# Score products of a gated linear recurrence: from full 128x128 blocks to 32x32 and 64x64 tiles

## The chip, the core and the metric

One core of one Trainium2 chip runs the whole kernel. The metric is device time in microseconds (us), the median of several runs; a smaller time is better. PE is TensorE's matmul side and PEld its weight loads, DVE is VectorE, ACT is ScalarE, POOL is GpSimd, SP is SyncE, whose queue issues the DMAs.

## The reference, cut to what matters

One layer of a hybrid trunk on 2048 latent tokens of width 1024 with 256 context tokens. A combined projection feeds two head groups, the outputs are projected back, and a gated MLP with a 3x3 depthwise convolution follows. The change is in the first head group: a gated linear recurrence in both directions, with four heads of 128 channels. For one direction it computes

```python
decay = jnp.where(mask, jnp.exp(jnp.where(mask, diff, 0.0)), 0.0)     # diff = b_t - b_s, b the running sum of log gates
scores = jnp.einsum('bhtk,bhsk,bhtsk->bhts', qc, kc, decay)
o = o_inter + jnp.einsum('bhts,bhsv->bhtv', scores, vc)               # o_inter: queries on the state before the chunk
```

The score of a query t and a key s is a sum over 128 channels of q, k and the product of the gates between them. Forward scores have s before t, backward ones t before s, and on the diagonal both directions add up.

## The kernel before, in words

**Scores level by level.** The kernel takes chunks of 128 positions, so a sequence half of 1024 positions (hh = 0 or 1) has eight. In a chunk the scores are made by halving: at level B (1, 2, 4, ... 64) positions are in blocks of B, two neighbouring blocks make a pair, and the scores between the two blocks of a pair are wanted. For these the decay splits into a part on the query side and a part on the key side, so that one plain matrix product gives them. `Q` holds the queries of the two directions, already decayed up to a block's edge, `K` likewise the keys; after each level `level_update` multiplies one half of `Q` by the totals of the blocks (in place, L470 of DVE), `level_keys` writes new keys (multiplications on DVE and POOL, L546 and L537, copies on ACT, L548 and L538), and `next_tot` the totals of the blocks twice as long. The diagonal comes first, from `kd = K[:,0] + K[:,1]` and plain queries `qs`.

**How a level is computed.** `hg` (L719) does this per head and half, so eight times. At each level each of the eight chunks gets one full 128x128 product in fp32 (the keys of the chunk as weights, a view of `Q` as the moving operand, L744), four to a bank of PSUM. Of its 128x128 results only the opposite blocks of the pairs are wanted; DVE copies those into `sc` through a byte mask of that level (`copy_predicated`, L747, 128x512 at a time). The diagonal's products (L731) come first and ACT copies them whole (L732). A product in fp32 is two passes of PE, each a weight load and a matmul; those in fp32r (the projections) are one. At the end `sc` is multiplied with the values (L795), beside the queries on the states.

**What sets the order.** PE's stream between 233 and 996 us is mostly the input projection, `run_banks` (L481): products of 128x512 in fp32r, three for each of eight slices of the contraction. After each slice it calls `slot`, which lets two pumps emit a step of work: `hg_q` (the recurrence) and `bg_q` (modulation blocks, the scaled output and down weights). A step ends with `yield` of a wait, and the next one comes when the model clock `T.t` (which adds up a price for each product, L64) has moved on that far: 4.2 model us between most levels. `need` forces steps ahead of it where the next head wants a buffer. A scheduler then places the emitted instructions on each engine's queue, and semaphores keep them correct. All engines work through their queues in order.

Of the kernel before, what the change touches and what calls it, by code (L numbers as in the profile page):

```python
# [9 lines left out]
F32 = mybir.dt.float32  # L10
F32R = mybir.dt.float32r
BF16 = mybir.dt.bfloat16
U8 = mybir.dt.uint8
# [5 lines left out]
P = 128  # L19
# [3 lines left out]
TH = SEQ // 2  # L23
NCH = TH // P
# [6 lines left out]
RH = TH // GW  # L31
EPS = 1e-6
LV = [1, 2, 4, 8, 16, 32, 64]
AL = 512


# [12 lines left out]
def view(t, off, dims):  # L49

    return bass.AP(t.tensor, t.offset + off, [list(t.ap[0])] + [list(d) for d in dims])


class Tensor:
# [5 lines left out]
    def matmul(self, out, lhsT, rhs, **kw):  # L60
        n = 1
        for _, count in rhs.ap[1:]:
            n *= count
        self.t += n / 2400 + 0.0135 if rhs.dtype == F32R else 2 * max(0.112, n / 1200 + 0.005)  # L64
        return self.engine.matmul(out, lhsT, rhs, **kw)  # L65

    def transpose(self, out, in_, identity):
# [5 lines left out]
def tile_trunk(ctx, tc, x, c, cx, c_ctx, w_ada, b_ada, norm_mix, norm_ffn, w_in, hg_norm, sgu_g, sgu_b,  # L73
               w_sp, b_sp, w_out, w_up, conv_w, conv_b, w_down, norm_final, masks, out):
    nc = tc.nc
    V, S, G, T = nc.vector, nc.scalar, nc.gpsimd, Tensor(nc.tensor)
    ld = nc.sync.dma_start
# [100 lines left out]
    with es1:  # L178
        ps = es1.enter_context(tc.tile_pool(name="ps1", bufs=1, space=PSUM, reuse_waits="tile"))
        p1 = es1.enter_context(tc.tile_pool(name="p1", bufs=1, reuse_waits="tile"))  # L180
        pm = es1.enter_context(tc.tile_pool(name="pm", bufs=1, reuse_waits="tile"))
        pk = esk.enter_context(tc.tile_pool(name="pk", bufs=1, side="right", reuse_waits="tile"))
        ph = esh.enter_context(tc.tile_pool(name="ph", bufs=1, side="right", reuse_waits="tile"))
        wa = [p1.tile([P, NK, TH], F32, tag=t, name="wa", align_bytes=AL) for t in ("xl", "xh")]
        wsT = pm.tile([P, NH, P], F32, name="wsT")
        rh = pm.tile([P, NH, P], F32, name="rh")
        msk = pm.tile([P, 8, P], U8, name="msk")
        hf = [pm.tile([P, P], F32, name=f"hf{h}") for h in range(NH)]
        hb = [pm.tile([P, P], F32, name=f"hb{h}") for h in range(NH)]
        tb0 = [pm.tile([P, NCH], F32, name=f"tb0_{h}") for h in range(NH)]  # L190
# [1 line left out]
        def bank(tag):  # L192
            return ps.tile([P, 512], F32, tag=tag, name=tag, bufs={"pj": 3, "sc": 2, "mi": 3}[tag])
# [230 lines left out]

        def misc():

            for l in range(0, 8, 4):
                mf = pm.tile([P, 4, P], F32, tag="gu", name="mf", bufs=2)
                ld(mf, masks.rearrange("p (l j) -> p l j", j=P)[:, l:l + 4, :])
                V.tensor_copy(msk[:, l:l + 4, :], mf)  # L430
            yield 1.0
            wsr = pm.tile([P, NH, P], F32, tag="nt", name="wsr", bufs=2)
            ld(wsr, w_sp[0].rearrange("h p q -> p h q"))
            bsb = pm.tile([P, NH, P], F32, tag="nt", name="bsb", bufs=2)
            ld(bsb, b_sp[0:1].broadcast_to([P, NH, P]))
            yield 5.0
            pv = bank("mi")
            for h in range(NH):
                T.transpose(pv[:, h * P:(h + 1) * P], wsr[:, h, :], ident)
            V.tensor_copy(wsT, pv.rearrange("p (h q) -> p h q", q=P))  # L440
            yield 2.5
            pv = bank("mi")
            for h in range(NH):
                T.matmul(pv[:, h * P:(h + 1) * P], ones, wsT[:, h, :], start=True, stop=True)
            for h in range(NH):
                V.scalar_tensor_tensor(out=rh[:, h, :], in0=pv[:, h * P:(h + 1) * P], scalar=sgb[:, h:h + 1],
                                       in1=bsb[:, h, :], op0=ALU.mult, op1=ALU.add)
            yield 0.0
# [162 lines left out]
        for h in range(NH):  # L611
            F, K, vt = sets[h % 2]
# [106 lines left out]
        def hg(hh, h, F, K, qs, vt, sgt):  # L719
            kd = ph.tile([P, TH], F32, tag="T1", name="kd")  # L720
            G.tensor_add(kd, K[:, 0, :], K[:, 1, :])
            Q = ph.tile([P, 2, TH], F32, tag="Q", name="Q", align_bytes=AL)
# [1 line left out]
                V.tensor_mul(Q[:, d, :], qs, F[:, d, :])  # L724
            yield 6.5
            sc = ph.tile([P, NCH, P], F32, tag="S", name="sc")
            for g in range(0, NCH, 4):
                pb = bank("sc")
                for i in range(4):
                    sl = slice((g + i) * P, (g + i + 1) * P)  # L730
                    T.matmul(pb[:, i * P:(i + 1) * P], kd[:, sl], qs[:, sl], start=True, stop=True)  # L731
                S.copy(sc[:, g:g + 4, :], pb.rearrange("p (c t) -> p c t", t=P))  # L732
            done.add((hh, h, "diag"))
            yield 3.6
            tot = F
            for l, B in enumerate(LV):
                dims = [[2 * B, P // (2 * B)], [TH + B, 2], [1, B]]
                if B == 1:
                    dims = dims[:2]
                if B == P // 2:  # L740
                    dims = dims[1:]
                for g in range(0, NCH, 4):
                    pb = bank("sc")
                    for i in range(4):  # L744
                        off = (g + i) * P
                        T.matmul(pb[:, i * P:(i + 1) * P], K[:, 0, off:off + P], view(Q, off, dims), start=True, stop=True)
                    V.copy_predicated(sc[:, g:g + 4, :], view(msk, l * P, [[0, 4], [1, P]]),  # L747
                                      pb.rearrange("p (c t) -> p c t", t=P))
                level_update(Q, TH, B, tot, False)
                K = level_keys(K, B, tot)  # L750
                tot = next_tot(tot, TH, B)
                yield (6.5, 5.2)[l] if hh == 0 and l < 2 else 4.2
# [16 lines left out]
            for d, dst, o in ((0, fs, 1), (1, bs_, 0)):  # L769
                for g in range(0, NCH, 4):  # L770
                    pd = bank("mi")
                    for i in range(4):
                        sl = slice((g + i) * P, (g + i + 1) * P)
# [15 lines left out]
            for g in range(0, NCH, 4):  # L789
                po = bank("mi")  # L790
                for i in range(4):
                    ch = g + i
                    sl = slice(ch * P, (ch + 1) * P)
# [266 lines left out]
        i = len(seq) - 4  # L1060
# [394 lines left out]
    for n, (u, i) in enumerate(prods):  # L1455
# [4 lines left out]
        p = ubank()  # L1460
# [275 lines left out]
```

## Time and profile before

| what | value |
|---|---|
| median of 3 runs | 2518.82 us (2515.85 to 2520.11) |
| profiled execution | 2518.86 us, its span 2517.0 us |
| busy share of the span | PE 97%, PEld 80%, DVE 72%, POOL 42%, ACT 38% |
| score products on PE | 896 + 128 passes, 138.0 us busy |
| masked copies L747 on DVE | 112, mean 739 ns, 81.0 us busy |
| stage with the recurrence | about 230 to 1010 us of the span |

In the page, a line of part 5 is a group of equal instructions with its count, busy time, mean duration in ns, the idle time of the engine ahead of them and what ended it. PE's instructions overlap in its pipeline, so a mean duration is longer than the distance between two starts; prices are read from starts. In the timeline the first number is the start and the second the time to the end of the last of the merged instructions, both in us.

### The profile page before, as it was taken

Reading aid. Unit: us, or ns where it says so; the run is one execution under the profiler, and the core shown is the slowest. Engines: PE = TensorE matmul, PEld = TensorE weight load, DVE = VectorE, ACT = ScalarE, POOL = GpSimd, SP = SyncE. Lnnn points to the kernel's source line nnn. Section 1 sums busy time; section 2 is a strip of 40 time slices with the busy share of each in tenths; the row PEclk is TensorE's granted clock in tenths of the full one; section 3 lists DMA queues with packets and bytes.
Section 4 is the critical chain, followed back from the end, with each engine's and each line's share of the span. In section 5 each row is a group of like instructions: output and inputs, shape, how many; then the busy total and the mean of one; then the engine's idle time right before and its main releaser. Section 6 shows DMA issues by size and latency. Waiting matters only on the chain.

```text
span 2517.0 us, 32793 instructions
## 1 busy us (share of the span) xinstructions
PE 2439.9 (97%) x11859; PEld 2021.6 (80%) x11859; DVE 1800.4 (72%) x2367; ACT 959.9 (38%) x1598; POOL 1060.6 (42%) x879
## 2 busy tenths in 40 slices
PE   7999999999999999899999999999999999999998
PEld 4788888878888888688778888878878887888887
DVE  5866766745757657365699787759999993675876
ACT  2554334434344333254443333323333342323243
POOL 1444232322333423100477878878778771000002
PEclk9999999999999999999999999999999999999999
DMA  8355334583342522667942222382222239843744
GB/s 293 101 193 174 116 113 159 176 295 112 126 158 97 176 85 76 234 204 235 313 140 89 86 87 90 104 307 73 91 91 90 87 113 332 294 150 126 257 138 176
DMA packets 305838, 400.13 MB, mean 159 GB/s; under 512 B 33025, under 2 KB 216057, under 8 KB 301965
## 3 DMA queue, kind: packets, MB, share of 16 engines
q1 hardware_dynamic: 302420, 397.30, 47.7%
q8 instruction: 94, 1.54, 0.3%
q10 hardware_dynamic: 3257, 0.75, 0.1%
q14 instruction: 67, 0.55, 0.1%
HBM read 288.85 MB, written 109.13 MB: 158 GB/s over the span
## 4 chain that ended last, share of the span: by engine, by line
PE 38%; DVE 6%; POOL 2%; issue 2%; DMA 2%; ACT 1%; SPq 0%; POOLq 0%; ACTq 0%; DVEq 0%
PE up L65 22%; PE dn L65 17%; DVE dn L1316 3%; DVE edges L1321 1%; POOL Al L121 1%; DMA raw<-in_w_up_dram 1%; DVE gp L1392 1%; ACT dn L1313 0%; DMA yfar<-yd 0%; POOL raw L1142 0%; DVE keep L1402 0%; DVE keep L1386 0%; DMA m<-cv 0%; ACT cv L1335 0%; POOL cv L1403 0%
## 5 line engine op out<-in xcount | busy, mean ns | idle before, releaser
L1316 DVE SCALAR_TENSOR_TENSOR dn<-gp,taps,dn 128x1024 f32<-128x1024 f32 x352 | 448.3, 1280 | 21.0 <-ACT dn L1313 17.8
L65 PE MATMUL up<-yfar,Ah 128*128 128x512 f32 x1232 | 394.4, 390 | 2.2 <-DMA yfar<-yd 2.2
L121 POOL TENSOR_TENSOR Al<-raw,Ah 128x512 fp32r<-128x512 f32 x264 | 343.9, 1311 | 90.1 <-ACT Ah L120 82.9
L65 PE MATMUL dn<-thl,mhl 128*128 128x512 f32 x1680 | 381.0, 389 | 0.0
L65 PE MATMUL pj<-xh,whi 128*128 128x512 f32 x896 | 366.8, 410 | 2.1 <-ACT whi L120 1.6
L65 PEld LDWEIGHTS dn<-thl,mhl 128*128 128x128 f32 x1680 | 315.2, 188 | 65.6 <-issue 0.2
L65 PE MATMUL pj<-xl,whi 128*128 128x512 f32 x896 | 353.6, 395 | 3.7 <-DMA xl<-xl_d 1.8
L65 PE MATMUL pj<-xh,wlo 128*128 128x512 f32 x896 | 353.4, 395 | 2.7 <-POOL wlo L121 1.7
L65 PE MATMUL up<-xah,Al 128*128 128x512 f32 x704 | 275.9, 392 | 2.4 <-POOL Al L121 2.4
L65 PE MATMUL up<-xah,Ah 128*128 128x512 f32 x704 | 275.2, 391 | 1.8 <-ACT Ah L120 1.8
L65 PEld LDWEIGHTS up<-yfar,Ah 128*128 128x128 f32 x1232 | 231.4, 188 | 50.8 <-DMA yfar<-yd 2.6
L120 ACT CAST Ah<-raw 128x512 fp32r<-128x512 f32 x264 | 160.4, 618 | 283.5 <-PE up L65 213.7
L121 POOL TENSOR_TENSOR wlo<-raw,whi 128x1024 fp32r<-128x1024 f32 x56 | 143.8, 2569 | 243.1 <-ACT whi L120 204.0
L65 PE MATMUL up<-xal,Ah 128*128 128x512 f32 x528 | 205.5, 389 | 0.0
L65 PE MATMUL up<-yfar,Al 128*128 128x512 f32 x528 | 205.2, 389 | 0.0
L65 PEld LDWEIGHTS pj<-xh,wlo 128*128 128x128 f32 x896 | 169.7, 189 | 39.5 <-POOL wlo L121 2.1
L65 PEld LDWEIGHTS pj<-xh,whi 128*128 128x128 f32 x896 | 170.0, 190 | 36.9 <-issue 3.8
L65 PEld LDWEIGHTS pj<-xl,whi 128*128 128x128 f32 x896 | 170.0, 190 | 36.1 <-DMA xl<-xl_d 2.8
L65 PE MATMUL dn<-wo,o 128*128 128x512 f32 x768 | 184.9, 397 | 3.4 <-DMA wo<-wo_d 2.1
L65 PEld LDWEIGHTS dn<-wo,o 128*128 128x128 f32 x768 | 143.0, 189 | 33.7 <-DMA wo<-wo_d 2.5
L65 PEld LDWEIGHTS up<-xah,Al 128*128 128x128 f32 x704 | 132.4, 188 | 33.8 <-POOL Al L121 6.4
L65 PEld LDWEIGHTS up<-xah,Ah 128*128 128x128 f32 x704 | 132.6, 188 | 30.2 <-ACT Ah L120 2.8
(320 smaller groups left out, 4077.3 us busy)
## 6 DMA issues: line engine op xcount, KB each, us to landing
raw<-in_w_up_dram SPq DMA_DIRECT2D x88, 512.0 KB
mr<-m SPq DMA_DIRECT2D x85, 512.0 KB
raw<-in_w_in_dram SPq DMA_DIRECT2D x68, 512.0 KB
sT<-wd SPq DMA_DIRECT2D x88, 256.0 KB
raw<-in_w_ada_dram SPq DMA_DIRECT2D x32, 512.0 KB
yfar<-yd SPq DMA_DIRECT2D x14, 1024.0 KB
m<-cv SPq DMA_DIRECT2D x22, 544.0 KB
raw<-in_w_down_dram SPq DMA_DIRECT2D x22, 512.0 KB
```

The costliest lines, as they stand in the source:

```text
L65: return self.engine.matmul(out, lhsT, rhs, **kw)
L120: keep(S.copy(hi, raw))
L121: (eng or G).tensor_sub(lo, raw, hi.bitcast(F32))
L1316: V.scalar_tensor_tensor(out=cr, in0=gt[:, t // 3:t // 3 + RH, t % 3:t % 3 + GW], scalar=taps[:, t * NF + f:t * NF + f + 1], in1=cr, op0=A ...
L1321: V.scalar_tensor_tensor(out=e[:, 0, :], in0=gt[:, 1, t % 3:t % 3 + GW], scalar=taps[:, t * NF + f:t * NF + f + 1], in1=e[:, 0, :], op0=AL ...
L1392: V.tensor_add(g_rows(hh, f + c, n2), quad(p, kind), quad(add, kind))
```

## The change

Only the wanted blocks are computed, as small tiles. A tile takes all 128 rows of the array (the channels) and 32 or 64 of its columns, at the column group that goes with the partitions of its result. For the diagonal and the levels below 32 (`B < SB`) each chunk gets four products 32x32 (keys and queries of the same 32 positions), and the results of all eight chunks lie packed in one bank, 128x256. ACT copies the diagonal's results into a packed tile `near`, DVE merges the levels 1 to 16 into it with a mask of 32 columns. At level 32 the four products of a chunk are the 32x32 blocks off the diagonal, at level 64 there are two of 64x64; ACT copies these into `sc` block by block, and with level 32 also the blocks of `near`. One bank is used per level in place of two. The model clock prices a tile at a share of a pass by its width, which holds for the one- and two-column products of the modulation too. The masks are loaded in four small DMAs in place of two.

```diff
 LV = [1, 2, 4, 8, 16, 32, 64]
+SB = 32
+NB_ = LV.index(SB)
...
-        self.t += n / 2400 + 0.0135 if rhs.dtype == F32R else 2 * max(0.112, n / 1200 + 0.005)
+        if lhsT.ap[1][1] < P and out.ap[0][1] == lhsT.ap[1][1]:
+            self.t += 2 * lhsT.ap[1][1] / P * max(0.03, n / 1200 + 0.005)
+        else:
+            self.t += n / 2400 + 0.0135 if rhs.dtype == F32R else 2 * max(0.112, n / 1200 + 0.005)
...
-        msk = pm.tile([P, 8, P], U8, name="msk")
+        msk = pm.tile([P, NB_, SB], U8, name="msk")
...
-            for l in range(0, 8, 4):
-                mf = pm.tile([P, 4, P], F32, tag="gu", name="mf", bufs=2)
-                ld(mf, masks.rearrange("p (l j) -> p l j", j=P)[:, l:l + 4, :])
-                V.tensor_copy(msk[:, l:l + 4, :], mf)
+            mf = pm.tile([P, NB_, SB], F32, tag="gu", name="mf", bufs=2)
+            for i in range(0, P, SB):
+                ld(mf[i:i + SB], masks.rearrange("p (l j) -> p l j", j=P)[i:i + SB, :NB_, i:i + SB])
+            V.tensor_copy(msk, mf)
...
             sc = ph.tile([P, NCH, P], F32, tag="S", name="sc")
-            for g in range(0, NCH, 4):
-                pb = bank("sc")
-                for i in range(4):
-                    sl = slice((g + i) * P, (g + i + 1) * P)
-                    T.matmul(pb[:, i * P:(i + 1) * P], kd[:, sl], qs[:, sl], start=True, stop=True)
-                S.copy(sc[:, g:g + 4, :], pb.rearrange("p (c t) -> p c t", t=P))
+            near = ph.tile([P, NCH, SB], F32, tag="near", name="near")
+
+            def scores(key, query, w, across, dims):
+
+                pb = bank("sc")[:, :NCH * w].rearrange("p (c t) -> p c t", t=w)
+                for c in range(NCH):
+                    for i in range(0, P, w):
+                        t = i + w - 2 * (i % (2 * w)) if across else i
+                        off = c * P + t + (t // w % 2 * TH if across else 0)
+                        T.matmul(pb[i:i + w, c, :], key[:, c * P + i:c * P + i + w], view(query, off, dims),
+                                 start=True, stop=True, tile_position=(0, i))
+                return pb
+            S.copy(near, scores(kd, qs, SB, False, [[1, SB]]))
             done.add((hh, h, "diag"))
             yield 3.6
             tot = F
             for l, B in enumerate(LV):
-                dims = [[2 * B, P // (2 * B)], [TH + B, 2], [1, B]]
-                if B == 1:
-                    dims = dims[:2]
-                if B == P // 2:
-                    dims = dims[1:]
-                for g in range(0, NCH, 4):
-                    pb = bank("sc")
-                    for i in range(4):
-                        off = (g + i) * P
-                        T.matmul(pb[:, i * P:(i + 1) * P], K[:, 0, off:off + P], view(Q, off, dims), start=True, stop=True)
-                    V.copy_predicated(sc[:, g:g + 4, :], view(msk, l * P, [[0, 4], [1, P]]),
-                                      pb.rearrange("p (c t) -> p c t", t=P))
+                if B < SB:
+                    dims = [[2 * B, SB // (2 * B)], [TH + B, 2], [1, B]]
+                    dims = dims[:2] if B == 1 else dims[SB == 2 * B:]
+                    pb = scores(K[:, 0, :], Q, SB, False, dims)
+                    V.copy_predicated(near, view(msk, l * SB, [[0, NCH], [1, SB]]), pb)
+                else:
+                    pb = scores(K[:, 0, :], Q, B, True, [[1, B]])
+                    for i in range(0, P, B):
+                        t = i + B - 2 * (i % (2 * B))
+                        S.copy(sc[i:i + B, :, t:t + B], pb[i:i + B])
+                        if B == SB:
+                            S.copy(sc[i:i + B, :, i:i + B], near[i:i + B])
                 level_update(Q, TH, B, tot, False)
```

How this stands on the engines is seen in two places. The first is PE at the levels 32 and 64 of head 3 of the first half, where the steps are forced and PE waits today (`pj` is the projection's bank, `sc` the scores' bank, `mi` the bank of the key transposes behind). Before:

```order
L65 MATMUL sc<-Q,K_4859 128x128 x8
L65 MATMUL pj<-xh,whi 128x512
L65 MATMUL pj<-xl,whi 128x512
L65 MATMUL pj<-xh,wlo 128x512
L65 MATMUL pj<-xh,whi 128x512
L65 MATMUL pj<-xl,whi 128x512
L65 MATMUL pj<-xh,wlo 128x512
L65 MATMUL pj<-xh,whi 128x512
L65 MATMUL pj<-xl,whi 128x512
L65 MATMUL pj<-xh,wlo 128x512
L65 MATMUL sc<-Q,K_4887 128x128 x8
```

The same place with the change, PE again:

```order
L70 MATMUL sc<-Q,K_5489 32x32 x32
L70 MATMUL pj<-xh,wlo 128x512
L70 MATMUL pj<-xh,whi 128x512
L70 MATMUL pj<-xl,whi 128x512
L70 MATMUL pj<-xh,wlo 128x512
L70 MATMUL pj<-xh,whi 128x512
L70 MATMUL pj<-xl,whi 128x512
L70 MATMUL sc<-Q,K_5538 64x64 x16
```

The bursts have become 32 and 16 products for 8, and six projection products stand between the two for nine. The second place is ACT at the end of head 0 of the second half, where the keys for level 32 (`K_5434` before, `K_6233` with the change), those for level 64 (`K_5489`, `K_6315`) and those to be transposed behind it (`K_5533`, `K_6368`) are copied; `sig` and `whi` belong to the projection. Before:

```order
L548 COPY K_5434<-K_5389 128x16x2x16 x2
L931 ACTIVATE sig<-pj 128x512
L548 COPY K_5489<-K_5434 128x8x2x32 x2
L120 CAST whi<-raw 128x1024
L931 ACTIVATE sig<-pj 128x512
L538 COPY K_5533<-K_5489 128x8x2x64
```

With the change, where `near` is the packed tile:

```order
L553 COPY K_6233<-K_6164 128x16x2x16 x2
L943 ACTIVATE sig<-pj 128x512
L553 COPY K_6315<-K_6233 128x8x2x32
L760 COPY sc<-near 32x8x32 x4
L553 COPY K_6315<-K_6233 128x8x2x32
L125 CAST whi<-raw 128x1024
L943 ACTIVATE sig<-pj 128x512
L758 COPY sc<-sc 32x8x32 x4
L543 COPY K_6368<-K_6315 128x8x2x64
```

The four copies of `near` now stand between the two copies that make level 64's keys, and the four of level 32's scores ahead of the copy of the keys to be transposed.

## Prediction

> **What bounds the kernel now.** I read the page's busy shares first, then the busy times of the stage in which the recurrence runs, then the groups of PE and its waits there, and last the timeline round single bursts. The page first:
>
> ```profile
> PE 2439.9 (97%) x11859; PEld 2021.6 (80%) x11859; DVE 1800.4 (72%) x2367; ACT 959.9 (38%) x1598; POOL 1060.6 (42%) x879
> ...
> PEclk9999999999999999999999999999999999999999
> ```
>
> TensorE is busy for 97% of the span, at a granted clock that stays in the top tenth. The score products lie between 233 and 996 us, so the stages of interest are two windows around that:
>
> ```profile
> core 0: us, PE busy (x) PEld busy (x) DVE busy (x) ACT busy (x) POOL busy (x), PEclk, DMA share, GB/s
> 230.00:640.00 410.00, 393.64 (x2141) 335.73 (x2141) 263.38 (x349) 156.55 (x232) 126.81 (x71) 0.98 0.50 163
> 640.00:1010.00 370.00, 361.06 (x2087) 313.07 (x2085) 244.74 (x370) 143.58 (x299) 132.57 (x92) 1.00 0.35 117
> ```
>
> PE is busy for 754.7 of these 780 us; DVE for 508, ACT for 300, POOL for 259. The stage is TensorE's: what its instruction stream loses or gains here moves the end, unless a wait fills it. The groups and PE's waits in these windows:
>
> ```profile
> L65 PE MATMUL sc<-Q,K 128*128 128x128 f32 x896 | 122.1, 291 | 12.0 <-DVE Q L470 8.8 <-ACT K L548 3.2
> L65 PE MATMUL sc<-qs,kd 128*128 128x128 f32 x128 | 15.9, 275 | 0.0
> ...
> PE sc L65 <- DVE Q L470: 8.8, 9, 1.8
> PE mi L69 <- ACT vv L555: 3.3, 3, 2.6
> PE sc L65 <- ACT K L548: 3.2, 2, 1.9
> ```
>
> There are 1024 score passes (512 products, each of two passes of a weight load and a product), and PE waits 12 us in all for the data of the next level. The busy time counts the modelled tail of each burst, so I take a burst's price from starts instead.
>
> **What is removed.** A usual level, then a head's first level (B = 1, where neighbours of the moving operand lie far apart):
>
> ```profile
> 256.52 0.40 PE L65 MATMUL pj<-xh,wlo 128*128 128x512 f32 x1
> 256.75 1.95 PE L65 MATMUL sc<-Q,K 128*128 128x128 f32 x16
> 258.45 0.47 PE L65 MATMUL pj<-xh,whi 128*128 128x512 f32 x1
> 258.76 0.39 PE L65 MATMUL pj<-xl,whi 128*128 128x512 f32 x1
> ...
> 239.60 2.82 PE L65 MATMUL sc<-Q,K 128*128 128x128 f32 x16
> 242.12 0.54 PE L65 MATMUL pj<-xh,whi 128*128 128x512 f32 x1
> 242.50 0.39 PE L65 MATMUL pj<-xl,whi 128*128 128x512 f32 x1
> ```
>
> Projection passes start 0.23 us apart (256.52 to 256.75). From the burst's first start to the second projection after it are 2.01 us; less 0.23 this is 1.78 us for 16 passes, 111 ns each. The first level takes 2.90 - 0.23 = 2.67 us, 167 ns a pass, half as much again. A head has eight bursts (one on the diagonal, seven levels): 7 x 1.78 + 2.67 = 15.1 us, and eight heads 121 us. This leaves PE's stream.
>
> **What is added on PE.** Each head now has 7 bursts of 32 products 32x32 and one of 16 products 64x64, still of two passes each: 448 passes of 32 columns and 32 of 64, 3840 in all for 1024. What sets a pass is seen where few columns meet many:
>
> ```profile
> 28.23 0.40 PE L69 MATMUL pj<-ident,rows 2*128 2x2 f32 x4 [1.06 <-DVE rows L270]
> 28.56 0.59 PE L65 MATMUL pj<-wa,cs 128*2 128x512 f32 x1
> ...
> 28.99 0.08 PEld L65 LDWEIGHTS pj<-wa,cs 128*2 128x2 f32 x1 [0.34 <-issue]
> 29.42 0.09 PEld L65 LDWEIGHTS pj<-wa,cs 128*2 128x2 f32 x1 [0.34 <-issue]
> 29.85 0.09 PEld L65 LDWEIGHTS pj<-wa,cs 128*2 128x2 f32 x1 [0.34 <-issue]
> ...
> L65 PEld LDWEIGHTS pj<-wa,cs 128*2 128x2 f32 x48 | 3.9, 89 | 22.6 <-issue 22.5
> L65 PEld LDWEIGHTS sc<-Q,K 128*128 128x128 f32 x896 | 117.8, 197 | 20.9 <-issue 13.6 <-ACT K L548 4.0
> ```
>
> 512 moving columns take 0.43 us, 0.84 ns each; a weight load grows by (197 - 89) / 126 = 0.86 ns a column. So 128 columns stream 107 ns, and a 111 ns pass is that and 4 more, its load hidden behind the pass before. By the same count a pass of 32 is 27 + 4 = 31 ns, a first-level one 46 (half as much again), a pass of 64 is 57 ns. If the passes run one after another, a head costs 6 x 64 x 31 + 64 x 46 + 32 x 57 ns = 16.7 us, eight heads 133 us: cutting the columns by four has been paid back by four times the passes, and nothing is gained. All hangs on whether products in different column groups run at the same time. No row shows two groups at work together (every small product here sits in the first group). The bounds: with all groups at once the 32-wide passes take a quarter (8 x 14.9 / 4 = 30 us) and the 64-wide half (8 x 1.8 / 2 = 7 us), 37 us; one after another 133 us; and at worst each load with its product needs its own time of issue. The densest pairs of small passes in the trace are the four of 28.23: from the first to 28.56 is 0.33 us, 0.09 of it the change of mode priced below, so 60 ns each, which would make 3840 x 60 = 230 us. I take the middle case, two at once: a product's two passes sit in the same group, next to each other in the program, so the second has to wait for the first's stream, while the next product's first pass, in the next group, can start beside it. That halves 133 to 67 us.
>
> **The change of mode.** The program also goes from whole-array passes to column tiles and back. The trace shows this price, in the one-column products of the ada blocks, which the built program places as tiles of 128 rows and 32 columns too:
>
> ```profile
> 253.99 0.39 PE L65 MATMUL pj<-xh,wlo 128*128 128x512 f32 x1
> 254.30 1.02 PE L65 MATMUL mi<-acc,ones 128*1 128x512 f32 x2
> 255.25 0.50 PE L65 MATMUL pj<-xh,whi 128*128 128x512 f32 x1
> 255.59 0.39 PE L65 MATMUL pj<-xl,whi 128*128 128x512 f32 x1
> ...
> 253.76 0.19 PEld L65 LDWEIGHTS pj<-xh,wlo 128*128 128x128 f32 x1
> 254.30 0.09 PEld L65 LDWEIGHTS mi<-acc,ones 128*1 128x1 f32 x2 [0.35 <-issue]
> 255.25 0.19 PEld L65 LDWEIGHTS pj<-xh,whi 128*128 128x128 f32 x1 [0.86 <-issue]
> ```
>
> The load of 254.30 isn't pulled ahead as that of 253.76 is (for the product of 253.99); the array empties first, about 0.09 us each way, and the first load after lies bare. From 253.99 to 255.59 are 1.60 us, for work of 0.23 + 2 x 0.43 + 0.23 = 1.32: 0.28 us, and 0.03 more as 32 columns load bare instead of one. With 64 bursts, of which two merge and some are cut, some 65 round trips: 20 us, all on PE.
>
> **What moves off DVE and onto ACT.** DVE loses 112 masked copies and gains 40 of half the width; ACT loses 16 copies and gains, in each head, one of 128x256, eight of 32x256 and two of 64x512.
>
> ```profile
> L747 DVE COPY_PREDICATED sc<-msk,sc 128x512 f32<-128x512 uint8 x112 | 81.0, 739 | 48.4 <-PE sc L65 47.7
> L470 DVE TENSOR_TENSOR Q<-Q,tot 128x1024 f32<-128x1024 f32 x48 | 67.5, 1406 | 0.0
> ...
> L732 ACT COPY sc<-sc 128x512 f32<-128x512 f32 x16 | 9.2, 587 | 11.5 <-PE sc L65 11.5
> L707 ACT COPY fs<-hf 128x128 f32<-128x128 f32 x8 | 2.4, 300 | 6.6 <-PE mi L65 6.6
> ```
>
> DVE: 81 us go, 40 x about 0.4 (half the width of 739 ns) = 16 come. It's busy 508 of 780 us, so the 65 us are worth only what PE waits for Q behind them: at most the 8.8 us above. ACT: between 300 ns for 128 and 587 for 512 a copy of 256 is about 395 ns; 9 x 395 + 2 x 587 = 4.7 us a head for 1.2, 28 us more in eight heads, beside 300 of 780. On the path are the four copies of near, ahead of the second key copy for which level 64 waits, and the four of level 32's scores, ahead of the copy for which the transposes wait: 4 x 0.4 = 1.6 us each, 25 us in eight heads at most, less where those key copies wait for DVE or POOL anyway. So the waits add between -12 (the 12 us all gone) and +25 us; I take 0, since today's 12 us are the nearest row and the two pull against each other. The two more mask loads on SP, in the context stage, and the smaller prices on the pumps' clock cost nothing that I can find: in the order the last w_down product of DVE (the fill-in work) still stands ahead of the last head's states, whose PE work hides it; were it late, one load and product of it would lie bare, some microseconds.
>
> **The sum**, against the profiled execution's 2518.86 us (span 2517.0; the median of the runs is 2518.82, the same): 2518.86 - 121 + 67 + 20 + 0 = 2485 us.
>
> **Rivals.** *One at a time* (the tiles don't do what they are for): 133 + 20 - 121 = +32, 2551 us. For it: nothing in the trace shows groups side by side. Against: nothing shows them held apart. It decides from 26 ns a pass, since (121 - 20) / 3840 us is what a pass may cost. *Each pair by itself*: load and product each need the sequencer, 60 ns a pass; 230 + 20 - 121 = +129, 2648 us. For it: the four passes at 28.23 are the densest pairs of the trace. Against: they load 128 columns, which may be what takes the 60 ns.
> The Trainium skill, "TensorE: Matmul & The Clock Gate", Part 3, has a rule that would bring this about by another way: a weight load overlaps products in flight only where the row groups differ, and here all tiles take all rows. The trace doesn't bear it out for the whole array: the load of 253.76 starts 0.23 us ahead of its product, while another runs. For column tiles no row shows it.
> *A floor per pass*: streams overlap across the groups, but a new pass starts only every 27 ns, its own bare stream, whatever its group and width: 3840 x 27 = 104, + 20 - 121 = +3, 2522 us, too little to tell.
> The Trainium skill, "TensorEngine Tiling (Array Packing)", Instruction Overhead, speaks against the change in this sense: a matmul has some 60 cycles of overhead, one column takes as long as 60, so no tiling factor should be taken from a dimension that is small already; with the 25 ns that "TensorE: Matmul & The Clock Gate", Part 1, gives for it the estimate would be 3840 x 25 = 96 us and 2514. No row of this trace has a pass this short.
> *All four at once*: 37 + 20 - 121 = -64, 2455 us.
>
> **How the numbers follow.** Two at once, with what lies round it (12 to 24 ns a pass), 0.42; all four 0.10; the floor 0.08; one at a time 0.22; each pair by itself 0.18. Within 0.2% (5 us), about what a measurement of this kernel can tell from no change, counts as the same. Faster 0.52, the same 0.08 (the floor), slower 0.40. The range leaves out the 60 ns case (0.18): from 2450 (all four, with some waits gone) to 2575 (one at a time, with ACT's 25 us). Both signs hold much of it; the forecast's own range is 2464 (3840 x 12 = 46) to 2510 (92).
>
> **What would show it.** Right: the starts of a 32x32 burst take about 1.06 us for its 64 passes, with 0.3 us round it; the score groups' busy time falls by a third or more; neighbouring products' starts alternate between near 30 ns and a few. Wrong: 2 us a burst (one at a time), near 4 (each pair by itself), or PE's waits for ACT's K at level 64 of over a microsecond a head.

## The result and the profile after

| | before | after |
|---|---|---|
| median of the runs | 2518.75 us (2515.85 to 2520.11) | 2484.36 us (2482.05 to 2486.68) |
| ratio of the times | | 0.9866, 95% interval 0.985 to 0.9882 |
| span of the profiled execution | 2517.0 us | 2483.1 us |

The change saves 34 us. In two later runs one execution had a granted clock of 0.67 (3286.87 us, widest distance) or 0.72 (4353.39 us, the kernel before beside the untied runs); it counts in the median but in no ratio. The forecast of 2485 stands within a microsecond of the result, but what it added on PE was 22 us too much and what it added for waits 26 us too little, and the two cancelled. I read the profile after in the order in which that comes out: the bursts, the waits, then the work that the waits are for.

**The bursts.** PE's timeline of the changed kernel round the diagonal and the first level of a head (start, time to the end of the last of the merged passes):

```profile
234.49 0.39 PE L70 MATMUL pj<-xh,wlo 128*128 128x512 f32 x1
234.81 0.76 PE L70 MATMUL sc<-qs,kd 128*32 128x32 f32 x64
235.50 0.50 PE L70 MATMUL pj<-xh,whi 128*128 128x512 f32 x1
235.84 0.39 PE L70 MATMUL pj<-xl,whi 128*128 128x512 f32 x1
...
239.82 0.89 PE L70 MATMUL sc<-Q,K 128*32 128x32 f32 x64
240.64 0.50 PE L70 MATMUL pj<-xh,whi 128*128 128x512 f32 x1
```

The 64 passes take 0.69 us up to the next projection (234.81 to 235.50), about 11 ns a pass with the last one's stream; the first level takes 0.82. The single starts in the trace show how. The first passes start at 234.808, 234.814, 234.821 and 234.828, and the second ones from 234.860 on: four groups start 6 to 7 ns apart, and each takes its next pass some 32 ns later (the trace doesn't name a pass's group; I read it from this pattern). All four column groups stream at once. A 64x64 burst takes about 1.1 us.

**The stage.** The busy times of the changed kernel in the same two windows as before (window, its length, then PE, PEld, DVE, ACT, POOL):

```profile
230.00:640.00 410.00, 380.32 (x3780) 306.28 (x3779) 250.78 (x322) 175.67 (x276) 139.60 (x75) 0.97 0.50 161
640.00:1010.00 370.00, 347.11 (x3400) 287.82 (x3398) 230.68 (x370) 155.87 (x348) 141.03 (x101) 0.98 0.43 145
```

Its score groups in the two windows together:

```profile
L70 PE MATMUL sc<-Q,K 128*32 128x32 f32 x3072 | 38.9, 202 | 21.0 <-DVE Q L475 11.3 <-ACT K L553 7.8 <-POOL K L551 1.9
L70 PE MATMUL sc<-Q,K 128*64 128x64 f32 x256 | 11.2, 248 | 3.1 <-DVE Q L475 2.7 <-POOL K L551 0.4
L70 PE MATMUL sc<-qs,kd 128*32 128x32 f32 x512 | 6.5, 199 | 1.2 <-POOL kd L726 1.2
```

And PE's waits there (us in total, times, the longest):

```profile
PE sc L70 <- DVE Q L475: 14.0, 10, 2.7
PE mi L74 <- ACT vv L560: 10.0, 5, 3.0
PE sc L70 <- ACT K L553: 7.8, 5, 4.0
...
PE sc L70 <- POOL K L551: 2.2, 2, 1.9
```

The score groups' busy time has fallen from 138 to 57 us, but PE is now busy for 727 of the 780 us instead of 755. It waits 14.0 us for Q (8.8 before), 10.0 for the copied values `vv` (3.3) and 10.0 for K (7.8 for ACT's and 2.2 for POOL's; 3.2 before).

**The account.** I compare the same stretch of the program, from the last projection pass ahead of the first score burst to the first output projection: 804.1 us before, 769.5 after, so 34.7 us saved (the windows' ends fall on other work in the two kernels). Starts of PE's passes give the parts:

| part of the stretch, us | before | after | change |
|---|---|---|---|
| score bursts, first start to the next other pass, stops taken out | 121.2 | 51.5 | -69.7 |
| going in (0.229, then 0.319) and out (0.315, then 0.336), 64 times | | | +7.1 |
| stops (distances between starts beyond those of steady work) | 36.4 | 59.3 | +22.9 |
| projection passes at half speed behind stops | 3.6 | 7.1 | +3.5 |

The sum is -36.2; the 1.5 us to 34.7 are small pieces that I don't place. Where a slow distance ends and a stop begins is a choice; another cut moves the stops by a microsecond or two. So about 26 of the 70 us that the bursts save are given back in stops and behind them.

**One place where it is given back.** The timeline of the changed kernel at level 2 of head 0 (in brackets the idle time before and what ended it):

```profile
240.85 2.41 POOL L126 TENSOR_TENSOR wlo<-raw,whi 128x1024 fp32r<-128x1024 f32 x1 [7.98 <-ACT whi L125]
...
242.24 3.10 DVE L475 TENSOR_TENSOR Q<-Q,F 128x1024 f32<-128x1024 f32 x1
...
243.22 4.48 POOL L551 TENSOR_TENSOR K<-K,F 128x512 f32<-128x512 f32 x1
...
245.20 0.71 DVE L880 SCALAR_TENSOR_TENSOR acc<-raw,cs,acc 128x512 f32<-128x512 f32 x1
...
247.73 1.15 ACT L553 COPY K<-K 128x512 f32<-128x512 f32 x1 [5.40 <-POOL K L551]
248.93 0.78 PE L70 MATMUL sc<-Q,K 128*32 128x32 f32 x64 [1.20 <-ACT K L553]
...
250.46 1.56 POOL L551 TENSOR_TENSOR K<-K,tot 128x512 f32<-128x512 f32 x1 [2.76 <-ACT K L553]
...
251.12 1.98 DVE L475 TENSOR_TENSOR Q<-Q,tot 128x1024 f32<-128x1024 f32 x1
252.05 0.67 ACT L553 COPY K<-K 128x512 f32<-128x512 f32 x1 [1.67 <-POOL K L551]
252.60 0.59 ACT L560 COPY vv<-pj 128x512 f32<-128x512 f32 x1
253.24 1.12 PE L74 MATMUL mi<-ident,vv 128*128 128x128 f32 x4 [2.63 <-ACT vv L560]
254.01 0.78 PE L70 MATMUL pj<-xh,whi 128*128 128x512 f32 x1
254.59 0.63 PE L70 MATMUL pj<-xl,whi 128*128 128x512 f32 x1
```

PE comes to the burst 1.2 us before ACT has copied the keys, which had waited for POOL's product of 4.48 us. Then it comes to the value transposes, and `vv` stands on ACT's queue behind the keys of the next level, which wait for POOL again. Behind the stop the projection passes start 0.58 us apart (254.01 to 254.59) instead of 0.23. The same product of POOL in the timeline of the kernel before, with DVE beside it and the copy behind it, and below it head 2 of that kernel and a `Q<-Q,F` with no POOL work beside it:

```profile
241.57 1.92 POOL L546 TENSOR_TENSOR K<-K,F 128x512 f32<-128x512 f32 x1 [9.05 <-ACT K L548]
241.82 1.43 DVE L747 COPY_PREDICATED sc<-msk,sc 128x512 f32<-128x512 uint8 x2
...
243.13 2.47 DVE L470 TENSOR_TENSOR Q<-Q,F 128x1024 f32<-128x1024 f32 x1
...
243.51 1.20 ACT L548 COPY K<-K 128x512 f32<-128x512 f32 x1 [0.44 <-POOL K L546]
...
444.65 1.94 POOL L546 TENSOR_TENSOR K<-K,F 128x512 f32<-128x512 f32 x1
445.26 3.44 DVE L470 TENSOR_TENSOR Q<-Q,F 128x1024 f32<-128x1024 f32 x1
...
552.33 2.19 DVE L470 TENSOR_TENSOR Q<-Q,F 128x1024 f32<-128x1024 f32 x1
```

The key copy comes 4.2 us later (247.73 for 243.51), for two reasons. 1.65 us are POOL's later start (243.22 for 241.57): on its queue `wlo<-raw,whi`, work for the projection, now stands ahead of the key product, where it stood behind. The other 2.6 us are the product's longer duration. Of two such products the one that starts second grows by about what is left of the first: at 445.26 DVE's came second and took 3.44 us for 2.19, POOL's 1.94 as ever. At 242.24 DVE's is second to `wlo` (3.10 us) and POOL's key product at 243.22 is second to DVE's, with another product of DVE (`acc`) behind it: 4.48 us for 1.92. In three of the eight heads before, POOL's key product came first and DVE's grew to 3.2 us and more; in four of the eight after, DVE's came first and POOL's grew, to 3.3 us and more. With the masked copies halved in width and number and the burst over sooner, DVE is at `Q<-Q,F` earlier. Between this burst and the next PE has 30 projection passes in both kernels, but it arrives sooner, since the burst itself is 1.7 us shorter (0.82 us to the next projection for 2.52): the cover is gone.

**What the waits are for.** DVE lost the masked copies (81.0 us, now 17.8) and is busy only 27 us less in these windows. Its level products got longer, and POOL's with them. The groups of the changed kernel (`Q<-Q,tot` took 1406 ns before):

```profile
L475 DVE TENSOR_TENSOR Q<-Q,tot 128x1024 f32<-128x1024 f32 x48 | 79.1, 1649 | 8.5 <-PE sc L70 8.5
L551 DVE TENSOR_TENSOR K<-K,tot 128x512 f32<-128x512 f32 x40 | 41.1, 1029 | 24.8 <-ACT K L553 22.6 <-POOL K L551 2.2
L753 DVE COPY_PREDICATED near<-msk,sc 128x256 f32<-128x256 uint8 x40 | 17.8, 445 | 26.3 <-PE sc L70 26.2
...
L551 POOL TENSOR_TENSOR K<-K,F 128x512 f32<-128x512 f32 x8 | 24.0, 3004 | 1.9 <-ACT K L553 1.9
```

The groups of the kernel before that were not shown yet:

```profile
L546 DVE TENSOR_TENSOR K<-K,tot 128x512 f32<-128x512 f32 x40 | 33.5, 839 | 12.2 <-ACT K L548 12.2
...
L546 POOL TENSOR_TENSOR K<-K,F 128x512 f32<-128x512 f32 x8 | 16.3, 2035 | 10.4 <-ACT K L548 10.4
```

The same instructions on the same shapes: Q +11.6 us, DVE's K +7.6, POOL's first K +7.7. In the single records a `Q<-Q,tot` with no POOL instruction beside it takes 1.21 us before and 1.22 after; one that overlaps an instruction of POOL takes 1.71 and 1.96 in the mean. Of the 48, 19 did so before and 28 after. What counts is which starts first. Of the 56 products `Q<-Q,tot` and `Q<-Q,F` of a kernel, those that start with no instruction of POOL under way keep their time, whatever POOL starts behind them (35 before, 23 after; in the mean within 0.01 us of 1.21 and 2.19). Those that start beside one under way (21 before, 33 after) grow by what is left of it less about 0.13 us, all but one. The old masked copies took 745 ns beside POOL and 734 alone.
The Trainium skill, "SBUF — State Buffer", Who interferes with whom, says that a DVE instruction with two inputs in SBUF contends with a GpSimd instruction that reads SBUF, and one with at most one such input doesn't. The trace agrees with both halves, by the numbers above.

### The profile page after: what moved, and what is told of

Read it like the earlier page. It is cut to its first block, busy times and chain, and to the rows that moved or that the text cites. A ratio compares the mean times of both kernels' runs of the same rounds, so it can differ in the third digit from the quotient of the medians.

```text
span 2483.1 us, 38405 instructions
## 1 busy us (share of the span) xinstructions
PE 2383.5 (96%) x14675; PEld 1943.9 (78%) x14675; DVE 1757.0 (71%) x2294; ACT 986.5 (40%) x1670; POOL 1070.5 (43%) x879
```

## Experiments

All ratios are to the kernel before as it was measured beside the run. Its median was 2519.04 us beside group after group, price, distance and block copies; 2515.42 beside two groups, `vv` by DVE, later transposes and these with the wider distance; 2516.73 beside the untied pair and the kernel before with two numbers; 2519.14 beside the widest distance. Across these four I compare ratios.

### Group after group

```diff
-                for c in range(NCH):
-                    for i in range(0, P, w):
+                for i in range(0, P, w):
+                    for c in range(NCH):
```

> The same tiles in another order: group by group (eight products in the first column group, then eight in the second, and so on) instead of round the groups. If the short bursts of the changed kernel come from neighbouring products sitting in different column groups, a 32x32 burst goes back to 64 passes of about 31 ns, 2.0 us for 0.69, and a 64x64 one to 1.8 for 1.08: 56 x 1.3 + 8 x 0.75 = 79 us more, some of it swallowed where PE waits anyway, 2540 to 2565 us. Rival: a pass of 32 columns is cheap by itself, whatever its neighbour's group; then bursts stay at 0.7 us and the time at 2484.

2519.82 us, ratio 1.0005 (0.9995 to 1.0015): the whole gain is gone. The same burst in this kernel's timeline:

```profile
235.64 0.39 PE L70 MATMUL pj<-xh,wlo 128*128 128x512 f32 x1
235.96 1.91 PE L70 MATMUL sc<-qs,kd 128*32 128x32 f32 x64
237.80 0.50 PE L70 MATMUL pj<-xh,whi 128*128 128x512 f32 x1
```

1.84 us for 64 passes (B = 1 2.38 us, 64x64 1.83). Within a group the starts are 31 or 32 ns apart, as estimated for a single pass of 32 columns; 64 of these would be 2.02 us, and it is less because where one group ends the next has already begun (see the last section). The same tiles, the same work and the same change of mode, only in another order: what the change gains comes from groups that run beside each other. The time is lower than expected because the bursts grew by 71.5 us and not 79 (123.0 for 51.5), while PE's stops fell from 59.3 to 32.0 us, under the 36.4 of the kernel before, and the half-speed passes by 5 us more.

The run also shows what brings DVE and POOL together. At the place of above, again with `wlo` ahead on POOL:

```profile
244.59 0.46 DVE L753 COPY_PREDICATED near<-msk,sc 128x256 f32<-128x256 uint8 x1 [0.97 <-PE sc L70]
244.80 1.93 POOL L551 TENSOR_TENSOR K<-K,F 128x512 f32<-128x512 f32 x1
244.93 3.90 DVE L475 TENSOR_TENSOR Q<-Q,F 128x1024 f32<-128x1024 f32 x1
```

DVE has the halved masked copies here too, but the copy waits for the longer burst, so POOL's key product comes first and keeps its 1.93 us. Over the eight heads it takes 2.01 us in the mean (3.00 with the change), and `Q<-Q,tot` 1.48 (1.65). So the halved copies alone don't turn the order; with the shorter bursts it turns.

### Two groups at a time

```diff
-                for c in range(NCH):
-                    for i in range(0, P, w):
+                for r, c in [(r, c) for r in range(0, P, 2 * w) for c in range(NCH)]:
+                    for i in (r, r + w):
```

> Edit: in a score burst the tiles of column groups 0 and 1 are run first, for all eight products, product by product, and then those of groups 2 and 3, so that never more than two groups have work; the 64x64 bursts have two groups in either kernel and stay as they are. Theory 'each group streams by itself, at 31 ns a pass, and all that have work run at once': a 32x32 burst takes half of the 1.84 us that it took with one group at a time, plus little: 0.95 to 1.05 us for 0.69, B = 1 1.2 to 1.3 for 0.82; 8 bursts of B = 1 by +0.4 and 48 others less those, 40, by +0.31 make +16 us on the bursts; waits give back about 0.4 of that as they did there (-6): 2494 (2490 to 2500). Rival 'a floor of some 8 ns for each pass, whatever the groups': as the changed kernel, 0.69 us and 2484 (2481 to 2488). Rival 'at most one group beside another in any order': would have shown 1.0 us in the changed kernel itself, and is out.

2487.85 us, ratio 0.9885 (0.9868 to 0.9902). A usual burst takes 1.04 us, one with B = 1 1.34:

```profile
239.59 1.41 PE L70 MATMUL sc<-Q,K 128*32 128x32 f32 x64
240.93 0.50 PE L70 MATMUL pj<-xh,whi 128*128 128x512 f32 x1
```

With 1.84, 1.04 and 0.69 us for one, two and four groups the time of a burst follows the number of groups that have work, and the floor of 8 ns a pass is out. The 1.04 us is what the forecast (17 ns a pass, 1.06) had taken for the change. The surprise is the price: in the stretch the bursts take 71.4 us here and 51.5 in the changed kernel, but the times differ by 0.0019 of the ratio, 5 us, with intervals that overlap, so the second step isn't clear of noise. From group after group to two at a time the bursts lose 51.6 us and stops grow by 16.1 (32.0 to 48.1); from there to all four they lose 19.9 and stops grow by 11.2. The faster the bursts, the less of it arrives.

### Price and distance of the steps

The model clock that spaces the steps charges a tile by its width. Charging it like an old product:

```diff
-        if lhsT.ap[1][1] < P and out.ap[0][1] == lhsT.ap[1][1]:
-            self.t += 2 * lhsT.ap[1][1] / P * max(0.03, n / 1200 + 0.005)
+        if "tile_position" in kw:
+            self.t += 2 * lhsT.ap[1][1] / P * 0.112
```

> The tiles as changed, but the pumps' model clock charges a level what it charged before (1.79 us), so that everything timed by that clock stands as before. If the 25 us of new waits come from the clock's smaller prices (steps emitted at other places, the value copy behind two key copies on ACT), they go: 2460 to 2470 us. If they come from the shorter time between two bursts, which the price of a burst doesn't touch, nothing changes: 2480 to 2490.

2491.12 us, 0.989 (0.9871 to 0.9908): not faster, and a microsecond above what the second case allowed. The wait on vv grew to 15.0 us; Q's stayed at 13.9.

The levels further apart:

```diff
-                yield (6.5, 5.2)[l] if hh == 0 and l < 2 else 4.2
+                yield (7.8, 6.5)[l] if hh == 0 and l < 2 else 5.5
```

> 1.3 model us more between levels (5.5 for 4.2, 7.8 and 6.5 for 6.5 and 5.2), about what a burst has become shorter, so the period from burst to burst is as before the change. If the new waits come from the shorter period (ACT, POOL and DVE can't make the next level's keys and queries in it), PE's waits for DVE Q, ACT K and ACT vv fall from 32 us towards the 15 of before and the time to 2462 to 2474 us. Rival: the longer spacing only pushes more levels into the forced steps at the heads' ends, where the same work is waited for: 2480 to 2495.

2487.23 us, 0.9878 (0.9863 to 0.9893). The waits changed places; PE's in this kernel:

```profile
PE mi L74 <- ACT vv L560: 14.8, 4, 4.8
PE sc L70 <- DVE Q L475: 9.7, 8, 2.3
PE sc L70 <- ACT K L553: 9.6, 4, 4.1
```

Q fell by about as much as vv rose, and the time is not to be told from that of the change. So neither the price nor the distance alone is what holds the rest of the gain.

### ACT's or DVE's hands

The block copies at levels 32 and 64 by DVE instead of ACT (both lines L758 and L760):

```diff
-                        S.copy(sc[i:i + B, :, t:t + B], pb[i:i + B])
+                        V.tensor_copy(sc[i:i + B, :, t:t + B], pb[i:i + B])
...
-                            S.copy(sc[i:i + B, :, i:i + B], near[i:i + B])
+                            V.tensor_copy(sc[i:i + B, :, i:i + B], near[i:i + B])
```

> The block copies into sc at levels 32 and 64 (four, four and two a head) on DVE instead of ACT. If these ACT copies cause the waits for ACT's keys and values (7.8 and 10.0 us), most of that goes: 2470 to 2478 us. If DVE's update of Q is the tighter one (14.0 us of waits), its copies ahead of it cost 1.6 us and more a head: 2485 to 2500. If neither binds there, no change.

2494.09 us, 0.9904 (0.989 to 0.9919), slower than the change, with vv still at 10.0, Q at 14.3 and K at 9.9: the copies that the change gave to ACT are not what makes K and vv late. The added stop is one for DVE's `tot`, 5.3 us (none with the change).

The copies `vv` by DVE:

```diff
-                S.copy(vc[:, :n], pj)
+                V.tensor_copy(vc[:, :n], pj)
```

> Edit: the copy of a projected value tile (vv) is done by DVE instead of ACT; its place in the order is the same. It tells whether vv waits because ACT's own queue holds it (a K copy that waits for POOL stands ahead of it) or because its projection is late. Theory 'ACT's queue': DVE works on the level's products there and takes the copy between two of them; the vv wait falls from 10.0 to under 4 us, DVE gets some 10 us more work, of which the waits on Q (14.0) take up to 5: time 2476 to 2484. Rival 'DVE is as full as ACT': the vv wait stays above 7 us or Q's grows by as much as vv's falls: 2484 to 2495.

2487.61 us, 0.9884 (0.9866 to 0.9902). The wait on vv fell to 4.4 us and that on Q rose to 21.4. Work that goes from ACT to DVE brought no gain in either run: with the block copies it cost time, with `vv` the 3 us more are within the noise. Of the two engines DVE is the one short of room.

### Later value transposes

```diff
-                hg_q.later(g, 2.2)
+                hg_q.later(g, 5.0)
```

> Edit: the four transposes of a value tile are put 5.0 us of planned TensorE time behind their projection instead of 2.2. Theory 'the wait on vv is a cost of its own': in the changed kernel TensorE stands 10.0 us for ACT's copies vv in the recurrence's stretch, and about ten matmul pairs behind each such stop start at twice the usual distance (about 4 us together). With the transposes later vv is copied before they come: the vv wait falls from 10.0 to under 2 us, the other waits stay within 3 us, and the time is 2484.4 - 10 - 4 = 2470 (2466 to 2475). Rival 'the waits only move': TensorE then reaches the next score burst sooner, and stands there for DVE's Q and ACT's K by as much more; vv near 0, Q and K together above 30 us (21.8 now), time 2480 to 2488.

2479.33 us, 0.9846 (0.9829 to 0.9864), against 0.9866 (0.985 to 0.9882) of the change: 5 us lower, with intervals that overlap. The wait on vv fell from 10.0 to 1.6 us as meant; Q rose from 14.0 to 16.8 and K from 10.0 to 11.1. Stops fell by 4.4 us in all. The time is in the rival's range, but Q and K together are 27.9 us and not above 30: about half of the wait moved.

With this, the wider distance of above as well:

> Edit: as the run before, and the planned distance between two levels 7.8, 6.5 and then 5.5 us instead of 6.5, 5.2 and 4.2. The wider distance alone lowered the wait on Q from 14.0 to 9.7 us and raised that on vv from 10.0 to 14.8, at 2487.2 us. Theory 'the wait on vv is a cost of its own': without it 2487.2 - 14.8 - 4 = 2468 (2464 to 2474), the lowest of the four. Rival 'the waits only move': the stops go to the heads' ends, where the levels that the wider distance put off are run without distance; time 2480 to 2490.

2473.34 us (2469.47 to 2474.77), 0.9824 (0.9806 to 0.9842): the fastest kernel of the study, and its interval lies below that of the change. PE's waits in it:

```profile
PE sc L70 <- ACT K L553: 9.7, 4, 4.1
PE sc L70 <- DVE Q L475: 7.3, 7, 2.0
...
PE mi L74 <- ACT vv L560: 3.6, 3, 1.9
```

Either edit alone moved waits into others (distance alone gained nothing, the later transposes alone 5 us by the ratio, within the noise); together they take 15.0 us of stops away. POOL's first key product still takes 3.13 us in this kernel and `Q<-Q,tot` 1.67, so the longer products needn't become stops where the plan leaves them room. Further apart still (9.1, 7.8 and 6.8 us):

> Edit: as the fastest run (value transposes 5.0 us behind their projection), and the levels 9.1, 7.8 and then 6.8 us apart instead of 7.8, 6.5 and 5.5. It tells how much of the waits is distance. Theory 'distance': the waits on Q (7.3 us) and K (9.7) that were left fall by half, with a microsecond or two of slow pitches: 2473.3 - 8.5 - 1.5 = 2463, a ratio to the kernel before of 0.977 to 0.980. Rival 'the other engines' work sets the pace of a head': what is put off runs together at the head's end, where TensorE stands for as long; 2470 to 2482, 0.981 to 0.986, with the waits on Q and K together at 15 us or more.

2478.32 us, 0.9837 (0.9824 to 0.9849), not to be told from the fastest run and not faster. Q is at 14.4 us and K at 5.5, 19.9 together: what is put off meets at the heads' ends, as the rival said.

The kernel before with the two numbers of the fastest kernel:

> The kernel before, with the two numbers of the fastest run so far: value transposes 5.0 us behind their projection, levels 7.8, 6.5 and 5.5 us apart. It tells whether those numbers answer to the new bursts or were simply better. Theory 'they answer to the new bursts': the kernel before stood 8.8 us for Q, 3.3 for ACT K, 3.3 for vv, and of these some 5 to 8 go: 2511 to 2514, a ratio of 0.997 to 0.999, where in the changed kernel the ratio moved by 0.0042 (0.9866 to 0.9824). Rival 'better for any kernel': the same 10 us, 0.996 or less.

2518.46 us, 1.0003 (0.9994 to 1.0012). It gains nothing, less than either case had expected. So the two numbers are not better in themselves; what they gain, they gain with the new bursts.

### TensorE untied from the levels

In the changed kernel and in the one before, the score passes read constants:

```diff
-                        T.matmul(pb[i:i + w, c, :], key[:, c * P + i:c * P + i + w], view(query, off, dims),
+                        T.matmul(pb[i:i + w, c, :], wsT[:, c % NH, i:i + w], rh[:, c % NH, i:i + w],
```

> The scores are left out of the result: in the changed kernel every pass of a score burst reads two constant arrays of the same kind (wsT and rh) in place of K or kd and Q or qs, with the same tile sizes, places and count. DVE, ACT and POOL still run every step of every level, but TensorE no longer waits for Q, K or kd, nor they for its passes. Theory 'the levels' chain ate the difference': the waits on Q (14.0 us), K (7.8 and 2.2) and kd (1.2) go, 25.2 us, with some 4 us of the slow pitches behind them; the wait on vv (10.0) stays: 2484.4 - 25.2 - 4 = 2455 (2448 to 2462). Rival 'the waits only move': TensorE stands instead for vv, o and nt, as long as before; 2475 to 2486.

> The same edit in the kernel before (128x128 products of the constant arrays; the scores are left out of the result): its waits on Q (8.8 us) and K (3.2) go, with perhaps 2 us of slow pitches: 2518.8 - 12 - 2 = 2505 (2500 to 2510). What it decides is the distance to the run with the new bursts: theory 'the levels' chain ate the difference' has what the bursts alone are worth, 121.6 - 55.3 - 12.7 = 53.6 us less what vv still takes back, 45 to 54 us (a ratio of 0.978 to 0.982 between the two); the rival, that the chain has no part in it, has the 34 us that the two kernels are apart now (0.9866).

2515.07 us, 0.9992 (0.9983 to 1.0001), and 2550.1 us, 1.0128 (1.0114 to 1.0141). Both are slower than with the ties, by about 32 us. No theory had that. PE's waits in the first:

```profile
PE mi L74 <- ACT vv L560: 26.6, 9, 7.6
PE sc L70 <- DVE near L753: 19.6, 6, 6.1
```

The edit did more than was meant. The scheduler places instructions by their dependencies, and without these it put DVE's and ACT's work in another order: at head 0 two Q products stand close together on DVE, and a row of `acc` products behind them, on whose loads DVE then waits (2.97 us at 246.68). So the pair doesn't isolate the levels' chain. Their ratio, 0.9992 / 1.0128 = 0.9866, is that of the change itself, where the chain theory wanted 0.978 to 0.982. The waits on Q and K went and others took their place, but since the order changed as well, the pair decides nothing about the chain.

## Why the prediction came out right

**What bounds the stage** was right: PE's stream was shortened and the time fell.

That the sum came within a microsecond is luck: every term of the sum missed, and the misses cancelled.

**What is removed**, 121 us, was 5 us too small. The trace has 121.2 us up to the next projection, but the prediction's price also counts the way out of the burst (0.315 us for a steady 0.229), another 5.5 us in 64 bursts. Most of the difference is three bursts at half clock (at 278.20, 369.50 and 875.91 us, 3.5 us together), which a price taken from two clean bursts doesn't hold.

**What is added on PE**, 67 us, is the step that failed: 51.5 us to the next pass. The 31 ns for a single pass hold (group after group: 31.6), and so does the reasoning by groups. The middle case rested on one sentence, that a product's second pass must wait for the first's stream while only the next product's first pass starts beside it. The starts show instead four groups under way at once (a burst takes 0.69 us where the prediction looked for 1.06); a pass that waits for its own group doesn't hold the passes of the others behind it. The right case was the rival with all four at once, to which 0.10 had been given. Its 37 us count no end of a burst: the last start lies 0.126 us ahead of the next projection, 8 us in 64 bursts.
The Trainium skill's rule that a load overlaps products only where the row groups differ ("TensorE: Matmul & The Clock Gate", Part 3) is not borne out for column tiles either: all tiles take all rows, and each of the 64 passes with its load takes about 11 ns. The same part also lets a load run ahead when it goes to the background weight buffer; the trace doesn't say where a load goes.
The estimate of 2514 us, worked out from the Trainium skill, "TensorEngine Tiling (Array Packing)", Instruction Overhead, is not borne out: across groups the starts are 6 to 7 ns apart. Within one group they are 31 or 32 ns apart, and in that order the change gains nothing (1.0005), as the advice has it.

**The change of mode**, 20 us, was too large: 0.09 us going in (0.319 for 0.229) and 0.11 coming out (0.336 for 0.229) make 0.20 us a burst, 13 us.

**DVE, ACT and the waits**, 0 us with ends at -12 and +25, came to +26: stops +22.9 and half-speed passes +3.5. It lies just past the upper end, and not by the mechanism priced there, so the 0 is the other step that failed. The block copies of ACT ahead of the late levels' keys are not it: given to DVE, vv stays at 10.0 and Q at 14.3, and before the 64x64 products PE waits 3.1 us in all, 2.7 of it for DVE's Q. The waits grew at Q, at early K copies and at vv. That the shorter bursts bring them is shown: the same tiles group after group have stops of 32.0 us for 59.3. How they do so is seen in single places: PE reaches the next level sooner than DVE, POOL and ACT finish it, and DVE's and POOL's level products lie beside each other more often and take longer. That DVE's 65 us of relief would be worth at most what PE waits for Q was right as a bound, and no gain from it is to be seen: its level products took back a good part beside POOL. How much of the 22.9 us is this slowing, how much the shorter cover and how much the other order on the queues stays open; no run took POOL's work away from beside DVE's, and none kept the old order with the new bursts.

So -121 + 67 + 20 + 0 was in the trace, with its own terms, about -126.7 + 51.5 + 12.6 + 26.4 = -36, for a measured 34.4: misses of 5.5, 15.5 and 7 us one way and of 26 the other. The 1.8 us between are the pieces not placed.

**The rivals.** One at a time was made real by the order of the tiles alone (1.84 us a burst) and is out for this one; the floor (27 ns a pass, 1.73 us a burst) and each pair by itself (60 ns, 3.8 us) are out by the 0.69 us.

## What to carry over

Small products in different column groups run side by side when they alternate in the program; put the groups in the inner loop, and count passes by group. When a change shortens the bursts of a paced pipeline, the work that feeds them gets the same time less to be ready: price that with the stops, and set the pacing anew, with its numbers together: here neither number alone cleared the noise, and both together did. Where a DVE product of two arrays and a POOL product meet, look which starts second, and give that one the rest of the other's time on top.

## What was not expected of the hardware

**Passes start out of the program's order.** In the run group after group the program has 16 passes of the first group, then those of the second. The starts and durations at the change (us, ns):

```
236.358 196
236.364 217
236.390 196
236.416 196
236.421 196
236.448 196
236.453 196
```

A pass of 217 ns is the first in its group (the burst's first pass has it, as have the first four in the changed kernel). 236.358 is the thirteenth pass, and the fourteenth to start already belongs to the second group; three more of the first, 32 ns apart (236.390, .421, .453), start behind it. The trace doesn't name the groups; this reading rests on the durations and distances alone. It goes against the sentence ahead of the prediction that all engines work through their queues in order: for passes of different column groups PE did not.

**Half speed behind a stop.** Behind longer stops (2.6 us at 253.24 and 2.4 us at 581.60) projection passes start 0.43 us apart instead of 0.23 for some microseconds. The mean granted clock of the core, 0.989, hides what the windows at these two places show (PEclk is the third number from the end):

```profile
251.95:258.78 6.83, 5.54 (x14) 3.65 (x15) 2.09 (x3) 2.86 (x5) 1.32 (x2) 0.50 0.20 73
583.04:586.46 3.42, 3.42 (x37) 2.58 (x35) 1.91 (x3) 2.09 (x5) 0.00 (x0) 0.50 0.51 182
```

The clock is granted at half there. The trace has 9 such stretches between 230 and 1010 us with the change, 37.5 us together; before there were 4 (20.5 us), in the run group after group 2 (6.8 us). All the slow distances lie in them, about 18 before, 36 after and 8 group after group, and each of the 9 begins during or within about 2 us behind a stop of 1.9 us or more. Not each such stop brings one: the 2.4 us ahead of 850.84 did not. So a stop can cost more than its own length.
